# Attention by pairs of key blocks: operations of 1024 columns over two PSUM banks

## The chip, the cores and the metric

The kernel runs on one core of a Trainium2 chip. The metric is the device time of one execution in microseconds (us), as the median of several runs. The core has a matrix engine (PE; its weight loads are shown apart as PEld), a vector engine (DVE), an activation engine (ACT), a general engine (POOL, GpSimd) and a queue for transfers (SP). Each works through its own list of instructions in order; semaphores tie the lists together. On-chip data lie in SBUF; matrix products land in PSUM, which has eight banks of 512 float32 columns on each of 128 partitions.

## The reference

Two layers on 2048 positions of width 1024: a Mamba-2 mixer, then latent attention with 16 heads. The change touches the attention alone:

```python
def causal_block_attention(q_nope, q_rope, k_nope, k_rope, v):
    S = q_nope.shape[1]
    scale = (QK_NOPE + QK_ROPE) ** -0.5        # 64 + 32 columns
    for i in range(S // Q_BLOCK):              # blocks of 128 queries
        ...
        s = einsum(q_nope, k_nope) + einsum(q_rope, k_rope)
        s = s.astype(jnp.float32) * scale
        mask = (q0 + local)[:, None] >= jnp.arange(kv_len)[None, :]
        p = jax.nn.softmax(jnp.where(mask, s, -jnp.inf), axis=-1).astype(v.dtype)
        outs.append(jnp.einsum('bhqk,bkhd->bqhd', p, v[:, :kv_len]))
```

Everything is float32 there. The kernel carries each operand as two float16 values, a high and a low half, and adds the products that matter.

## The kernel before

The stage works on 64 jobs: 16 heads, and in each the four quarters of 512 queries (`qb` = 0 to 3). The quarter `qb` needs 4*qb + 4 blocks of 128 keys. There are two passes over the scores.

*Maxima.* `maxima` (L1226) multiplies 128 queries by up to 512 keys, high halves only, into a PSUM bank (L1235), adds the causal mask on the last piece (L1237), and DVE reduces it to a maximum per query (L1238). After the job's last piece DVE forms the bias: the maximum over the pieces (`m`, L1243), its scaling (`me`, L1247), and its high and low half (`nm`, L1249 and L1250). `row` (L1252) turns these on PE (L1255), DVE copies them out (`rT`, L1257), and two transfers put them as two further rows behind the queries, so that the scores of the second pass come out with the maximum subtracted.

*Scores and values.* A unit is one block of 128 keys against the job's 512 queries. `scores` (L1261) makes three products into one bank (L1269 to L1271, high by high, high by low, low by high) and the mask on the diagonal (L1273). ACT takes the exponential (`x`, L1275) and copies it to float16, the high half (`PTs`, L1277). The low half is the difference (L1279): DVE makes it, or POOL in two of five units off the diagonal. `values` (L1282) multiplies, for each of four tiles of 128 queries, the high half by 130 columns (64 of the values' low half, 64 of their high half, 2 constant for the sum; L1291) and the low half by 66 of them (L1293), into two columns ranges of one tile `tr`. `finish` (L1301) runs twice per job: ACT copies one range (`Ot`, L1306), DVE takes the reciprocal of the sum (L1308) and adds the ranges (L1310), POOL multiplies (L1313). `store` (L1318) transposes a finished pair of heads (L1323), and ACT copies it out (L1325).

*What sets the order.* PE's order is written out by the loop at L1342: in each step i as many pieces of `maxima` as `due[i]` asks, then what waits in `later` (`row` after ROWS steps, `store` after TURN steps), then `scores` of unit i, then `values` of the unit HELD steps before. READY says how many units ahead of a job its maxima must be made. The lists of DVE, ACT and POOL are set by a scheduler that works from the same program. PSUM is shared by two groups of four banks: `mm` for maxima, scores, `row` and `store`, and `tr` for the outputs; buffers of a group are taken in turn.

After the stage, `back` (L1366) does the output product; its weight splits (L1383 on ACT, L1384 on POOL) are partly placed inside the attention stage.

Of the kernel before, what the change touches and what calls it, by code (L numbers as in the profile page):

```python
# [27 lines left out]
NH = 16  # L28
# [39 lines left out]
class Net:  # L68
# [1115 lines left out]
    def attention(self):  # L1184
        with ExitStack() as ctx:
            self.wo = self.tail.enter_context(self.tc.tile_pool(name="wo", bufs=1, side="right", reuse_waits="tile"))
            self.wraw = []
            sp = ctx.enter_context(self.tc.tile_pool(name="asp", bufs=2, reuse_waits="tile"))
            with self.tc.manual_schedule(engines={mybir.EngineType.PE}):
                self.heads(sp)  # L1190

    def heads(self, sp):
# [5 lines left out]

        def cuts(kv):

            out, at = [], 0
            while at < kv:
                w = min(TB, kv - at)
                if kv - at == TB + P:
                    w = 384
                out.append((at, w))
                at += w
            return out

        jobs = [(h, qb) for h in range(NH) for qb in range(NB)]  # L1210
        chunks, ends = [], []
        for n, (h, qb) in enumerate(jobs):
            for j in range(4):
                parts = cuts(qb * TB + (j + 1) * P)
                chunks += [(n, j, i, c0, w, i == len(parts) - 1) for i, (c0, w) in enumerate(parts)]
            ends.append(len(chunks))
        units = [(n, kb) for n, (h, qb) in enumerate(jobs) for kb in range(4 * qb + 4)]

        need = [ends[units[min(i + READY, len(units) - 1)][0]] for i in range(len(units))]
        due = list(need)  # L1220
        for i in range(len(units) - 2, -1, -1):
            due[i] = max(due[i], due[i + 1] - (2 if i < 40 and i % 2 else 1))

        peak, outs, pairs = {}, {}, {}

        def maxima(n, j, i, c0, w, last):  # L1226

            h, qb = jobs[n]
            if (j, i) == (0, 0):
                peak[n] = self.t(sp, "mx", [P, 4, 4], bufs=3)  # L1230
# [3 lines left out]
            s = self.t(self.pp, "mm", [P, TB], bufs=4)  # L1234
            mm(s[:, :w], Q[0:96, 0, qs], K[0:96, 0, c0:c0 + w], start=True, stop=not last)  # L1235
            if last:
                mm(s[:, w - P:w], self.idb, self.mk, start=False, stop=True)  # L1237
            v.tensor_reduce(peak[n][:, j, i:i + 1], s[:, :w], AX.X, ALU.max)  # L1238
            if last and j == 3:
                m = peak.pop(n)  # L1240
                if qb:
# [5 lines left out]
                v.tensor_scalar(e, x, -1.0 / MSCALE, LN16 / MSCALE, ALU.mult, ALU.add)  # L1247
                u = turned[n % 2]
                v.tensor_copy(u[:, 0:4], e)  # L1249
                v.tensor_tensor(u[:, 4:8], e, u[:, 0:4], ALU.subtract)  # L1250

        def row(n):  # L1252

            ps = self.t(self.pp, "mm", [P, TB], bufs=4)
            mm(ps[:, 0:P], turned[n % 2], self.idb, start=True, stop=True)  # L1255
            r = self.t(sp, "rT", [8, P], F16, bufs=2)
            v.tensor_copy(r, ps[0:8, 0:P])  # L1257
# [3 lines left out]
        def scores(i):  # L1261

            n, kb = units[i]
            h, qb = jobs[n]
            jj = max(kb - 4 * qb, 0)
            diag = kb >= 4 * qb
            Q, K, ks, c = quer[h, qb], keys[h % 2], slice(kb * P, (kb + 1) * P), slice(jj * P, TB)
            s = self.t(self.pp, "mm", [P, TB], bufs=4)
            mm(s[:, c], K[0:98, 0, ks], Q[0:98, 0, c], start=True, stop=False)  # L1269
            mm(s[:, c], K[0:96, 0, ks], Q[0:96, 1, c], start=False, stop=False)  # L1270
            mm(s[:, c], K[0:96, 1, ks], Q[0:96, 0, c], start=False, stop=not diag)  # L1271
            if diag:
                mm(s[:, jj * P:(jj + 1) * P], self.mk, self.idb, start=False, stop=True)  # L1273
            x = self.t(sp, "x", [P, TB], bufs=4)
            act(x[:, c], s[:, c], AF.Exp)  # L1275
            u = self.t(sp, "PTs", [P, 2, TB], F16, bufs=HELD + 2)
            act(u[:, 0, c], x[:, c], AF.Copy)  # L1277
            engine = nc.gpsimd if not diag and i % 5 in (1, 3) else v
            engine.tensor_tensor(u[:, 1, c], x[:, c], u[:, 0, c], ALU.subtract)  # L1279
            return u  # L1280

        def values(i, u):  # L1282

            n, kb = units[i]
            h, qb = jobs[n]
            V = vals[h % 2]
            if kb == 0:
                outs[n] = [self.t(self.pp, "tr", [P, 2, 256], bufs=4) for _ in range(2)]
            for j in range(max(kb - 4 * qb, 0), 4):
                o, js = outs[n][j // 2][:, j % 2], slice(j * P, (j + 1) * P)  # L1290
                mm(o[:, 0:130], u[:, 0, js], V[:, kb, :], start=kb == 0 and j % 2 == 0, stop=False,  # L1291
                   skip_group_check=True)
                mm(o[:, 64:130], u[:, 1, js], V[:, kb, 64:130], start=False, stop=kb == 4 * qb + j,  # L1293
                   skip_group_check=True)
            if kb in (4 * qb + 1, 4 * qb + 3):
                finish(n, (kb - 4 * qb) // 2)
            if kb == 4 * NB - 1 and h + 2 < NH:
                self.load_k(h + 2, 0, NB)
                self.load_v(h + 2)

        def finish(n, i):  # L1301

            h, qb = jobs[n]
            O = outs[n][i]
            t = self.t(sp, "Ot", [P, 2, 64], bufs=2)
            act(t, O[:, :, 0:64], AF.Copy)  # L1306
            ri = self.t(sp, "ri", [P, 2], bufs=2)
            v.reciprocal(ri, O[:, :, 128])  # L1308
            o = self.t(sp, "Oa", [P, 2, 64], bufs=2)
            v.tensor_tensor(o, O[:, :, 64:128], t, ALU.add)  # L1310
# [4 lines left out]
            if i and h % 2:  # L1315
                later.append((step[0] + TURN, lambda: store(h, qb)))

        def store(h, qb):  # L1318

            op = pairs.pop((h // 2, qb))  # L1320
            ps = self.t(self.pp, "mm", [P, TB], bufs=4)
            for j in range(4):
                nc.tensor.transpose(ps[:, j * P:(j + 1) * P], op[:, j].rearrange("p h d -> p (h d)"), self.ident)  # L1323
            o = self.t(sp, "Os", [P, TB], bufs=2)
# [14 lines left out]
                    later.remove((at, f))  # L1339
                    f()  # L1340

        for i in range(len(units)):  # L1342
            step[0] = i
            while made < due[i]:
                maxima(*chunks[made])
                made += 1
                n = chunks[made - 1][0]
                if made == ends[n]:
                    if i:
                        later.append((i + ROWS, lambda n=n: row(n)))  # L1350
                    else:
                        row(n)
            waiting()
            held.append((i, scores(i)))
            if len(held) > HELD:
                values(*held.pop(0))
        while held:
# [120 lines left out]
    def run(self):  # L1478
        tc = self.tc
        with ExitStack() as whole:  # L1480
            cp = whole.enter_context(tc.tile_pool(name="const", bufs=1))
            dp = whole.enter_context(tc.tile_pool(name="dram", bufs=1, space=DRAM))
            self.pp = whole.enter_context(tc.tile_pool(name="pp", bufs=4, space=PSUM))
# [18 lines left out]
            self.wo_d = dp.tile([G, 2, 2, P, 2, 2, TB], F16, name="wo_d")  # L1502
            self.xq = whole.enter_context(tc.tile_pool(name="xq", bufs=8, side="right"))
            self.layers()
            self.attention()
            self.back()
            self.tail.close()


# [48 lines left out]
```

## Time and profile before

| | |
|---|---|
| median of 3 runs | 3019.27 us (3012.62 to 3020.14) |
| the profiled run's own time | 3012.66 us |
| its span | 3010.9 us |
| attention stage, about | 2008 to 2824 us of the span |
| busy in the whole span | PE 95%, DVE 76%, ACT 63%, POOL 22% |
| granted clock over the span | 0.987 |

The profile is of one execution; what lies around its span is 1.8 us. Times in rows are microseconds from the span's start. A row of the timeline has start, duration, engine, line, operation, out<-in, the tile's shape, and in brackets the idle time before it with what ended it. Instructions of one engine overlap at their ends, so from start to start is less than the duration. A group of the page or of a window gives busy time and the mean in ns of one, then idle time ahead with its releasers. For PE the row's end is modelled; the starts are what to subtract.

### The profile page before, as it was taken

What the parts mean: (1) busy time and instruction counts of PE and PEld (TensorE: products, weight loads), DVE (VectorE), ACT (ScalarE), POOL (GpSimd) and SP (SyncE); (2) the same over time, 40 slices, a digit from 0 to 9 for tenths busy, and PEclk for the clock granted to TensorE, in tenths of its full rate; (3) what the DMA queues carried; (4) which work ended last, traced back from release to release, by engine and by line L of the source; (5) the groups of instructions that cost most, each with busy time, mean ns of one, the idle gap of its engine ahead of it and who ended that gap; (6) DMA issues with size and microseconds to landing.
All of it is one profiled execution on the core that took longest, in us unless ns stands there. A gap on an engine that the chain in (4) does not pass through costs nothing.

```text
span 3010.9 us, 55172 instructions
## 1 busy us (share of the span) xinstructions
PE 2871.6 (95%) x19726; PEld 1686.8 (56%) x19726; DVE 2281.5 (76%) x5162; ACT 1885.9 (63%) x4360; POOL 665.7 (22%) x798
## 2 busy tenths in 40 slices
PE   7899999999999999999999999989999999998998
PEld 3456656555555554544555454545666656665787
DVE  6789987787877788787855544368988989898554
ACT  8777666665766666565543433338888888887622
POOL 0212122121222112221111212113232323234200
PEclk9999999999999999999999999999999999999999
DMA  8765435544464456455357555631212121222462
GB/s 284 241 227 179 155 116 196 175 154 141 168 212 157 145 175 198 172 165 186 123 162 262 176 167 194 201 96 43 62 43 69 43 62 43 69 64 74 141 210 105
DMA packets 234248, 440.70 MB, mean 146 GB/s; under 512 B 59218, under 2 KB 101010, under 8 KB 232532
## 3 DMA queue, kind: packets, MB, share of 16 engines
q1 hardware_dynamic: 222836, 401.24, 41.9%
q0 software_dynamic: 11136, 35.92, 3.3%
q8 instruction: 155, 2.54, 0.3%
q14 instruction: 121, 0.99, 0.1%
HBM read 332.73 MB, written 104.34 MB: 145 GB/s over the span
## 4 chain that ended last, share of the span: by engine, by line
PE 60%; DVE 19%; ACT 10%; issue 6%; DMA 4%; POOL 1%; SPq 0%; ACTq 0%; DVEq 0%; POOLq 0%
PE mm L84 11%; PE mm L86 11%; PE mm L85 11%; PE tr L85 4%; PE tr L84 4%; PE tr L86 4%; DVE cacc L612 4%; ACT x L1275 3%; DVE PTs L1279 3%; DVE mx L1238 3%; ACT PTs L1277 2%; PE mm L1269 2%; PE mm L1270 2%; PE mm L1271 2%; PE tr L1291 2%
## 5 line engine op out<-in xcount | busy, mean ns | idle before, releaser
L1275 ACT ACTIVATE x<-mm 128x512 f32<-128x512 f32 (+3 forms) x640 | 336.1, 525 | 124.9 <-PE mm L1271 59.2
L1238 DVE TENSOR_REDUCE mx<-mm 128x1 f32<-128x512 f32 (+3 forms) x640 | 378.4, 602 | 39.3 <-PE mm L1237 23.4
L1277 ACT ACTIVATE PTs<-x 128x512 f16<-128x512 f32 (+3 forms) x640 | 361.7, 566 | 16.2
L1279 DVE TENSOR_TENSOR PTs<-x,PTs 128x512 f16<-128x512 f32 (+3 forms) x512 | 306.9, 604 | 45.3 <-ACT PTs L1277 35.2
L84 PE MATMUL mm<-xT,wsp 128*128 128x512 f16 x800 | 306.7, 383 | 6.3 <-ACT wsp L115 4.2
L85 PE MATMUL mm<-xT,wsp 128*128 128x512 f16 x800 | 305.7, 382 | 0.0
L86 PE MATMUL mm<-xT,wsp 128*128 128x512 f16 x800 | 305.3, 382 | 0.0
L1291 PE MATMUL tr<-K,PTs 128*128 128x130 f16 x2176 | 280.0, 222 | 0.0
L1293 PE MATMUL tr<-K,PTs 128*128 128x66 f16 x2176 | 260.5, 194 | 9.0 <-POOL PTs L1279 6.2
L1291 PEld LDWEIGHTS <-PTs 128*128 128x128 f16 x2176 | 203.8, 98 | 61.4 <-issue 4.5
L84 PE MATMUL mm<-wsp,xT 128*128 128x512 f16 (+1 forms) x640 | 230.3, 361 | 4.7 <-ACT craw L606 4.5
L85 PE MATMUL mm<-wsp,xT 128*128 128x512 f16 (+1 forms) x640 | 230.5, 360 | 3.2 <-DVE wsp L116 3.2
L612 DVE SCALAR_TENSOR_TENSOR cacc<-craw,pack,cacc 128x512 f32<-128x512 f32 x288 | 214.1, 771 | 24.2 <-ACT cacc L610 23.2
L1269 PE MATMUL mm<-xT,K 98*128 98x512 f16 (+3 forms) x640 | 227.2, 355 | 4.3 <-DVE mx L1238 3.4
L1293 PEld LDWEIGHTS <-PTs 128*128 128x128 f16 x2176 | 197.7, 98 | 59.7 <-POOL PTs L1279 7.9
L86 PE MATMUL mm<-wsp,xT 128*128 128x512 f16 (+1 forms) x640 | 230.5, 360 | 0.0
L1270 PE MATMUL mm<-xT,K 96*128 96x512 f16 (+3 forms) x640 | 227.1, 355 | 0.0
L1235 PE MATMUL mm<-K,xT 96*128 96x512 f16 (+3 forms) x640 | 225.2, 358 | 1.1 <-DVE Xp L116 1.1
L1271 PE MATMUL mm<-xT,K 96*128 96x512 f16 (+3 forms) x640 | 225.6, 352 | 0.0
L802 POOL TENSOR_TENSOR Xp<-Xw,Xp 128x512 fp32r<-128x512 f32 x64 | 89.6, 1400 | 499.6 <-ACT Xp L801 280.5
L84 PE MATMUL mm<-wsp,yT 128*128 128x512 f16 (+1 forms) x512 | 197.5, 386 | 2.2 <-DVE sz L636 1.6
L86 PE MATMUL mm<-wsp,yT 128*128 128x512 f16 (+1 forms) x512 | 195.8, 382 | 0.0
(461 smaller groups left out, 6946.9 us busy)
## 6 DMA issues: line engine op xcount, KB each, us to landing
wsp<-wi_d SPq DMA_DIRECT2D x96, 512.0 KB
big<-cumT SPq DMA_DIRECT2D x64, 512.0 KB
wraw<-in_ssm_w_out_dram SPq DMA_DIRECT2D x96, 256.0 KB
wi_d<-wsp SPq DMA_DIRECT2D x32, 512.0 KB
wsp<-wo_d SPq DMA_DIRECT2D x32, 512.0 KB
wsp<-wu_d SPq DMA_DIRECT2D x28, 512.0 KB
hx<-in_ssm_w_in_dram SPq DMA_DIRECT2D x48, 256.0 KB
wraw<-in_ssm_w_in_dram SPq DMA_DIRECT2D x48, 256.0 KB
```

The lines of the kernel that those rows point to most:

```text
L84: mm(out, l_hi, r_hi, start=start, stop=False)
L85: mm(out, l_hi, r_lo, start=False, stop=False)
L86: mm(out, l_lo, r_hi, start=False, stop=stop)
L612: nc.vector.scalar_tensor_tensor(acc, raw[:, k:k + TB], wk[k], acc, ALU.mult, ALU.add)
L1238: v.tensor_reduce(peak[n][:, j, i:i + 1], s[:, :w], AX.X, ALU.max)
L1269: mm(s[:, c], K[0:98, 0, ks], Q[0:98, 0, c], start=True, stop=False)
L1270: mm(s[:, c], K[0:96, 0, ks], Q[0:96, 1, c], start=False, stop=False)
L1275: act(x[:, c], s[:, c], AF.Exp)
L1277: act(u[:, 0, c], x[:, c], AF.Copy)
L1279: engine.tensor_tensor(u[:, 1, c], x[:, c], u[:, 0, c], ALU.subtract)
L1291: mm(o[:, 0:130], u[:, 0, js], V[:, kb, :], start=kb == 0 and j % 2 == 0, stop=False, skip_group_check=True)
L1293: mm(o[:, 64:130], u[:, 1, js], V[:, kb, 64:130], start=False, stop=kb == 4 * qb + j, skip_group_check=True)
```

## The change

A unit becomes a pair of key blocks. The two blocks' scores lie in two neighbouring banks, the second block's pushed to the start of its bank so that the columns are contiguous, and Exp and Copy run once over up to 1024 columns. The low half of the first block is made by DVE, that of the second by POOL, in every pair. Maxima are reduced over up to 1024 columns, so a job has one piece or two per 128 queries. The value product of 130 columns becomes one of 64 and one of 65, all three now accumulating into the same 65 columns; `finish` runs once per job, with a reciprocal and one multiplication by DVE out of PSUM. PSUM in this stage is three buffers of two banks (`s`, for maxima, scores, `row`, `store`) and two banks for outputs (`o`). HELD, READY, ROWS and TURN count pairs now. The bank groups before and after the stage are opened apart.

```diff
-HELD = 3
-READY = 7
-ROWS = 2
-TURN = 4
+HELD = 2
+READY = 4
+ROWS = 1
+TURN = 2
...
         def cuts(kv):
-            out, at = [], 0
-            while at < kv:
-                w = min(TB, kv - at)
-                if kv - at == TB + P:
-                    w = 384
...
+            first = kv if kv <= 2 * TB else TB if kv <= 3 * TB else 2 * TB
+            return [(0, first)] + ([(first, kv - first)] if kv > first else [])
...
-            due[i] = max(due[i], due[i + 1] - (2 if i < 40 and i % 2 else 1))
+            due[i] = max(due[i], due[i + 1] - (3 * TB if i < 20 else 2 * TB))
...
+        def bank():
+            return self.t(self.ap, "s", [P, 2, TB], bufs=3)
...
-                    v.tensor_reduce(x, m[:, :, :qb + 1], AX.X, ALU.max)
+                    v.tensor_tensor(x, m[:, :, 0], m[:, :, 1], ALU.max)
...
+            x = self.t(sp, "x", [P, 2 * TB], bufs=3)
+            act(x[:, at:end], s, AF.Exp)
+            u = self.t(sp, "PTs", [P, 2, 2 * TB], F16, bufs=HELD + 2)
+            act(u[:, 0, at:end], x[:, at:end], AF.Copy)
+            v.tensor_tensor(u[:, 1, at:TB], x[:, at:TB], u[:, 0, at:TB], ALU.subtract)
+            nc.gpsimd.tensor_tensor(u[:, 1, TB:end], x[:, TB:end], u[:, 0, TB:end], ALU.subtract)
...
-                mm(o[:, 0:130], u[:, 0, js], V[:, kb, :], start=kb == 0 and j % 2 == 0, stop=False,
-                   skip_group_check=True)
-                mm(o[:, 64:130], u[:, 1, js], V[:, kb, 64:130], start=False, stop=kb == 4 * qb + j,
-                   skip_group_check=True)
+                    hi, lo = u[:, 0, at:at + P], u[:, 1, at:at + P]
+                    mm(o[:, 0:64], hi, V[:, k, 0:64], start=k == 0 and j == 0, stop=False, skip_group_check=True)
+                    mm(o[:, 0:65], hi, V[:, k, 64:129], start=False, stop=False, skip_group_check=True)
+                    mm(o[:, 0:65], lo, V[:, k, 64:129], start=False, stop=k == 4 * qb + j, skip_group_check=True)
...
-            act(t, O[:, :, 0:64], AF.Copy)
...
-            nc.gpsimd.tensor_tensor(pairs[h // 2, qb][:, 2 * i:2 * i + 2, h % 2, :], o,
-                                    ri.unsqueeze(2).to_broadcast([P, 2, 64]), ALU.mult)
+            v.reciprocal(ri, O[:, :, 64])
+            v.tensor_tensor(pairs[h // 2, qb][:, :, h % 2, :], O[:, :, 0:64],
+                            ri.unsqueeze(2).to_broadcast([P, 4, 64]), ALU.mult)
```

What it does to the engines' lists, at three places. First PE, one query tile's value products before:

```order
L1291 LDWEIGHTS PTs_22211
L1291 MATMUL tr_22104<-K_3813_20590,PTs_22211 128x130
L1293 LDWEIGHTS PTs_22211
L1293 MATMUL tr_22104<-K_3813_20590,PTs_22211 128x66
L1291 LDWEIGHTS PTs_22211
L1291 MATMUL tr_22104<-K_3813_20590,PTs_22211 128x130
```

and after the change (line numbers of the changed kernel):

```order
L1299 LDWEIGHTS PTs_22034
L1299 MATMUL o_22075<-K_3813_20590,PTs_22034 128x64
L1300 LDWEIGHTS PTs_22034
L1300 MATMUL o_22075<-K_3813_20590,PTs_22034 128x65
L1301 LDWEIGHTS PTs_22034
L1301 MATMUL o_22075<-K_3813_20590,PTs_22034 128x65
```

Two loads and two products have become three and three, the high half being loaded twice. Second DVE, from the last maximum of a fourth quarter to the copy of its row, before (L1238 maximum, L1243 to L1250 the bias, L1279 a low half, L1257 the copy):

```order
L1238 TENSOR_REDUCE mx_23663<-mm_24007 128x1
L1243 TENSOR_REDUCE m_24011<-mx_23663 128x4
L1247 TENSOR_SCALAR me_24013<-m_24011 128x4
L1238 TENSOR_REDUCE mx_24034<-mm_24039 128x1
L1249 CAST nm_4004_21660<-me_24013 128x4
L1250 TENSOR_TENSOR nm_4004_21660<-me_24013,nm_4004_21660 128x4
L1279 TENSOR_TENSOR PTs_24023<-x_24021,PTs_24023 128x512
L1238 TENSOR_REDUCE mx_24034<-mm_24060 128x1
L1257 CAST rT_24066<-mm_24064 8x128
```

and after, where the maximum is L1240, the bias L1245 to L1252, low halves L1282, the quarter's end L1313 and L1316, the copy L1259:

```order
L1282 TENSOR_TENSOR PTs_23774<-x_23772,PTs_23774 128x512
L1313 RECIPROCAL ri_23825<-o_23692 128x4
L1316 TENSOR_TENSOR Op_23827<-o_23692,ri_23825 128x4x64
L1240 TENSOR_REDUCE mx_23549<-s_23829 128x1
L1282 TENSOR_TENSOR PTs_23812<-x_23810,PTs_23812 128x512
L1245 TENSOR_TENSOR m_23834<-mx_23549 128x4
L1249 TENSOR_SCALAR me_23836<-m_23834 128x4
L1251 CAST nm_4004_21664<-me_23836 128x4
L1252 TENSOR_TENSOR nm_4004_21664<-me_23836,nm_4004_21664 128x4
L1259 CAST rT_23880<-s_23878 8x128
```

A low half stands between the last maximum and the bias now, and no maximum of the next job inside the bias. Third DVE, at a first quarter's four maxima, before:

```order
L1238 TENSOR_REDUCE mx_24034<-mm_24060 128x1
L1257 CAST rT_24066<-mm_24064 8x128
L1238 TENSOR_REDUCE mx_24034<-mm_24087 128x1
L1279 TENSOR_TENSOR PTs_24076<-x_24074,PTs_24076 128x512
L1238 TENSOR_REDUCE mx_24034<-mm_24109 128x1
L1279 TENSOR_TENSOR PTs_24098<-x_24096,PTs_24098 128x512
L1247 TENSOR_SCALAR me_24113<-mx_24034 128x4
```

and after:

```order
L1282 TENSOR_TENSOR PTs_23893<-x_23891,PTs_23893 128x512
L1282 TENSOR_TENSOR PTs_23932<-x_23930,PTs_23932 128x512
L1240 TENSOR_REDUCE mx_23999<-s_24004 128x1
L1282 TENSOR_TENSOR PTs_23971<-x_23969,PTs_23971 128x256
L1240 TENSOR_REDUCE mx_23999<-s_24008 128x1
L1240 TENSOR_REDUCE mx_23999<-s_24012 128x1
L1240 TENSOR_REDUCE mx_23999<-s_24016 128x1
L1249 TENSOR_SCALAR me_24020<-mx_23999 128x4
```

The four maxima, which were spread among the low halves of four units, now come in one step, with the last low half of the job before between the first and the second.

More of the change, by code (lines that the diff above doesn't have):

```diff
@@ L1233, in maxima @@
             Q, K, qs = quer[h, qb], keys[h % 2], slice(j * P, (j + 1) * P)
[L1234 to L1237, printed above, removed]
+            s = bank().rearrange("p a b -> p (a b)")
+            for at in range(0, w, TB):
+                c = min(TB, w - at)
+                diag = last and at + c == w
+                mm(s[:, at:at + c], Q[0:96, 0, qs], K[0:96, 0, c0 + at:c0 + at + c], start=True, stop=not diag)
+                if diag:
+                    mm(s[:, w - P:w], self.idb, self.mk, start=False, stop=True)
             v.tensor_reduce(peak[n][:, j, i:i + 1], s[:, :w], AX.X, ALU.max)
@@ L1264, in scores @@
             h, qb = jobs[n]
[L1265 to L1279, printed above, removed]
-            return u
-        def values(i, u):
-            n, kb = units[i]
+            Q, K, s = quer[h, qb], keys[h % 2], bank()
@@ L1504, in run @@
             self.layers()
+            banks.close()
             self.attention()
+            self.pp = banks.enter_context(tc.tile_pool(name="pe", bufs=4, space=PSUM, reuse_waits="tile"))
             self.back()
+            banks.close()
             self.tail.close()
```

89 lines of the change are left out of this document (50 added, 39 removed).

## The prediction

> **What bounds the kernel now.** I read the busy times of the attention stage first, then the waits, then single rows. The change touches only this stage, so its stretch is what counts (columns: stretch, length, busy time and instructions of PE, PEld, DVE, ACT, POOL, granted clock, DMA share, GB/s).
>
> ```profile
> 2010.00:2824.00 814.00, 743.74 (x7581) 484.74 (x7579) 724.31 (x1689) 683.69 (x1447) 250.05 (x262) 0.97 0.22 54
> ```
>
> PE 91%, DVE 89%, ACT 84%: no engine is clear of the next. The table of waits (engine, line, releaser: us, times, longest) says which wait ends last:
>
> ```profile
> PEld L1255 <- DVE nm L1250: 68.4, 62, 2.5
> PE mm L1255 <- DVE nm L1250: 52.7, 47, 2.2
> PE tr L1293 <- POOL PTs L1279: 6.2, 4, 2.1
> PE mm L1269 <- DVE mx L1238: 3.4, 10, 0.6
> ```
>
> PE stops almost only at `row`, L1255, for the DVE chain that turns the row maxima into biases: 68.4 us from the weights' side, 4.3 us per head. Nothing else stops it for long. The clock of 0.97 costs about 3% of 814, 24 us. The rest is PE's own work, so time comes from shorter PE work, shorter stops, or a steadier clock. These PE rows give its prices and the worst stop:
>
> ```profile
> 2330.52 0.38 PE L1269 MATMUL mm<-xT,K 98*128 98x512 f16 x1
> 2330.74 0.38 PE L1270 MATMUL mm<-xT,K 96*128 96x512 f16 x1
> ...
> 2338.69 0.22 PE L1291 MATMUL tr<-K,PTs 128*128 128x130 f16 x1
> 2338.75 0.19 PE L1293 MATMUL tr<-K,PTs 128*128 128x66 f16 x1
> 2338.78 0.22 PE L1291 MATMUL tr<-K,PTs 128*128 128x130 f16 x1
> ...
> 2339.04 0.33 PE L1235 MATMUL mm<-K,xT 96*128 96x384 f16 x1
> ...
> 2315.61 0.38 PE L1235 MATMUL mm<-K,xT 96*128 96x512 f16 x1
> 2318.08 0.23 PE L1255 MATMUL mm<-idb,nm 128*128 128x128 bf16 x1 [2.08 <-DVE nm L1250]
> ```
>
> 512 columns take 0.22 from start to start. Four value pairs of 130 and 66 columns take 2339.04 - 2338.69 = 0.35, 87 ns each, of which the short product is 0.03. Before 2318.08 PE stood 2.25 us beyond its last product's 0.22: DVE has other work between the links of the bias chain there.
>
> **The change, part by part.**
>
> *Short products.* Per block and query tile 130 + 66 columns become 64 + 65 + 65, each with its own weight load (2176 more pairs of load and product). At 29 ns each three are 87 ns: no change; by rounding +1 ns, +2 us. Ends: 57 ns each, the gap of the 130-column product, would add 2176 x (171 - 87) = +183 us; nothing makes them cheaper than 194/196 of now (-2 us). I take +2, since 66 columns with a load before them are measured and 64 or 65 are the nearest thing to them. The Trainium skill, "TensorE: Matmul & The Clock Gate", Back-to-back issue gap, gives about 81 ns for each load-and-product pair of 128 columns in a stream; by it 6528 pairs would be bound by loads and the sum some 2176 x 81 = 176 us higher. The trace has 57 ns at 130 columns, so the trace does not agree, and it stands only in the third rival.
>
> *ACT.* Two Exp and two Copy of 512 become one each of 1024.
>
> ```profile
> L1277 ACT ACTIVATE PTs<-x 128x512 f16<-128x512 f32 x448 | 282.1, 630 | 10.7
> L1275 ACT ACTIVATE x<-mm 128x512 f32<-128x512 f32 x447 | 263.9, 591 | 72.3 <-PE mm L1271 59.2 <-DVE PTs L1279 7.2 <-PE mm L1273 3.3
> L1277 ACT ACTIVATE PTs<-x 128x128 f16<-128x128 f32 x64 | 19.8, 309 | 2.0
> L1383 ACT ACTIVATE W<-wr 128x1024 fp32r<-128x1024 f32 x4 | 4.2, 1052 | 0.0
> L1306 ACT ACTIVATE Ot<-tr 128x128 f32<-128x128 f32 x128 | 34.6, 271 | 0.3 <-PE tr L1293 0.3
> ```
>
> From 128 to 512 columns a Copy grows by 321 ns, so 512 more columns cost 0.43 and 1024 take 1.06 (the 1024-wide row says 1.05); an Exp likewise about 1.02. One pair of blocks then holds ACT for 2.0 instead of 2.3 us: 320 x 0.3 = 96 us, and Ot's 35 go too. But of PE's waits for ACT the view shows less than 1 us, so this is worth nothing by itself. What it does is lengthen each link: from scores to low halves an Exp and a Copy now last 2.1 us instead of 1.2.
>
> *DVE.* 640 maxima become 384.
>
> ```profile
> L1238 DVE TENSOR_REDUCE mx<-mm 128x1 f32<-128x512 f32 x392 | 264.2, 682 | 15.4 <-PE mm L1235 14.6 <-PE mm L1237 0.3
> L1279 DVE TENSOR_TENSOR PTs<-x,PTs 128x512 f16<-128x512 f32 x320 | 226.6, 708 | 34.4 <-ACT PTs L1277 26.8 <-ACT x L1275 0.3
> L1279 POOL TENSOR_TENSOR PTs<-x,PTs 128x512 f16<-128x512 f32 x128 | 149.5, 1168 | 192.2 <-issue 110.3 <-ACT PTs L1277 74.1 <-PE tr L1293 4.1
> 2334.48 0.68 DVE L1238 TENSOR_REDUCE mx<-mm 128x1 f32<-128x512 f32 x1
> 2335.08 0.68 DVE L1279 TENSOR_TENSOR PTs<-x,PTs 128x512 f16<-128x512 f32 x1
> ```
>
> A 512-wide maximum is 0.68, and the next operation starts 0.60 after it did. One of 128 columns lasts 0.28 (further below), so a column costs 1.05 ns and one of 1024 columns holds DVE 1.14. Fewer starts save 256 x 0.07 = 18 us. The low halves lose what POOL takes over, and the outputs are finished in one piece. In sum about 4 us per head leave DVE: again only worth what it does to the stop.
>
> *POOL and the SBUF port.* Now POOL takes the second block's low half of every pair (320 instead of 128 operations), and DVE the first block's, both released by the same Copy. Before, unmasked blocks were divided between them in turn. Here are rows where the two met late in the stage:
>
> ```profile
> 2709.70 1.28 DVE L1279 TENSOR_TENSOR PTs<-x,PTs 128x512 f16<-128x512 f32 x1 [1.08 <-ACT PTs L1277]
> 2711.51 1.03 DVE L1279 TENSOR_TENSOR PTs<-x,PTs 128x512 f16<-128x512 f32 x1
> ...
> 2708.08 2.35 POOL L1384 TENSOR_TENSOR W<-wr,W 128x1024 fp32r<-128x1024 f32 x1 [1.46 <-ACT W L1383]
> 2710.40 1.60 POOL L1279 TENSOR_TENSOR PTs<-x,PTs 128x512 f16<-128x512 f32 x1
> ```
>
> DVE's low half begins at 2709.70 under POOL's operation and ends at 2710.98, 0.55 after that one does; POOL's next takes 1.60 while DVE finishes, and DVE's next at 2711.51 ends 0.54 after POOL's. They exclude each other: a pair costs POOL's 1.17 plus 0.54 in a row, not side by side. The bias chain is caught the same way:
>
> ```profile
> 2335.50 0.63 ACT L1277 ACTIVATE PTs<-x 128x512 f16<-128x512 f32 x1
> 2336.26 1.16 POOL L1279 TENSOR_TENSOR PTs<-x,PTs 128x512 f16<-128x512 f32 x1 [1.44 <-ACT PTs L1277]
> 2336.60 0.85 DVE L1247 TENSOR_SCALAR me<-m 128x4 f32<-128x4 f32 x1
> 2337.36 0.28 DVE L1238 TENSOR_REDUCE mx<-mm 128x1 f32<-128x128 f32 x1
> 2337.56 0.15 DVE L1249 CAST nm<-me 128x4 f16<-128x4 f32 x1
> 2337.75 0.16 DVE L1250 TENSOR_TENSOR nm<-me,nm 128x4 f16<-128x4 f32 x1
> ```
>
> A four-column operation lasts 0.85, to POOL's end at 2337.42; reductions out of PSUM pass freely. The Trainium skill's "GPSIMD Engine Reference", Specifications, says that GpSimd shares its SBUF interfaces with VectorE and contends with instructions that have two SBUF inputs; the rows agree, 1.60 beside 1.16. That rule speaks against this change.
>
> In the steady middle of a quarter this fits: PE needs 0.44 + 1.31 + 0.70 = 2.45 us per pair, the port 1.7, and the maximum runs under POOL. At the ends of jobs it does not. I laid the new orders out by hand over one head, starting each instruction at its releaser's end plus the gaps above (Copy's end at 2336.13 to POOL's start 0.13, a dependent DVE step 0.2, and by estimate 0.2 from the last score product's turn to Exp). Two places:
>
> Row of the fourth quarter: time 0 is the last maxima product. PE reaches `row` after 0.49 + 1.30 (scores) + 0.70 (values) = 2.5. On DVE, between the last maximum and the bias stands a low half. Its scores ended at -0.26 (nine short products before time 0), so Exp runs from -0.06 and Copy ends at 2.05; POOL takes its half from 2.18 to 3.34. DVE had to wait for POOL in the previous pair until 0.89, then needs 0.53 for that half, 0.53 for finishing the quarter before and 1.14 for the maximum: free at 3.09, it waits for POOL and ends at 3.87; four dependent steps of 0.2 give 4.7. PE waits 2.2, or 1.7 where the low half goes first by 0.1 us. By the same count: first quarter 0, second and third 1.3 each. Rows thus cost 4.3 to 4.8 per head, about as before: the shorter DVE work is eaten by the port.
>
> Score buffers: four single-bank buffers become three of two banks, and `row` and `store` take whole ones. At the first quarter's four maxima, which come together, the fourth product needs the first's buffer and the scores the second's; in DVE's order the second maximum stands behind a low half that waits for its Copy and POOL: 1.0 us. Then two pairs that wait for maxima (0.6 and 0.3), two that wait until DVE has copied `row`'s buffer, behind another low half (0.45 and 0.47), and two smaller ones of 0.3: together 3.4 per head. Before, the waits show 3.4 us for such buffers in the whole stage; that is the lower end, the upper is 3.4 more per head if all ties go wrong.
>
> *The rest.* The end of the stage gains 3 us: no product on POOL before the last transposes, and fewer starts on ACT. POOL's weight splits (L1384, above) now always stand before a low half; before, values waited 6.2 us for POOL, and I keep that. DMAs are the same in number; `row` to first scores keeps 6 us of PE work (5.4 before, where nothing waited; both counted in the order at the prices above), so this stays hidden; if it did not, each late job would cost the remainder. The clock I leave at 0.97: stops of about 2 us remain one per head.
>
> Sum: +2 (products) + 16 x (3.4 + 0 to 0.5 - 0.3 for small waits now gone) = +50 to +58, - 3 (end): +49 with ties in its favour. The profiled run took 3012.66, so 3062. That run stands 6.6 below the median of 3019.27, at the lowest of the three; I add 2 for that: **3064**.
>
> **Rivals.** *The port is dodged* (faster). DVE is lighter, so if it idles when a Copy ends, its half goes first by 0.09 us; POOL's late end then hides behind the two pairs held back, and bias and buffers come early. For it: DVE has 4 us less per head. Against: a 1.14 us maximum is in its way in most pairs. The same layout without the port gives rows of 0, 0.5, 0.7 and 1.1 us, 2.3 per head, and buffer waits of 2; with no stop near 2 us the clock would recover some 20: 16 x (4.3 - 4.3 - 0.3) - 20 + 2 - 3 = -26, about 2989 with the same 2 for the runs, and less where buffers come early too. It decides when POOL goes first in fewer than about a third of the pairs.
>
> *Nothing on the path moves* (same). ACT and DVE save beside PE, and new buffer waits equal what rows lose: 3012 to 3019. For it: the ends of jobs are few; against: waits of 3.4 per head would have to vanish exactly into 3.4 saved.
>
> *Short products do not stream* (slower still). Eight triples in a row, with a load each, are not in the trace. Each ns over 29 costs 6.5 us; at 35 ns it is +39, near 3100; at 57 each it is +183, near 3250. Against: the 0.03 rows above. The 81 ns that the Trainium skill gives for a stream of loads and products lies at that end; I leave 0.01 of this case's chance for it.
>
> **How the numbers follow.** First case 0.63 (own range 3030 to 3105), dodged port 0.22 (2955 to 3005), nothing moves 0.10, slow products 0.05. A change under 0.3%, 9 us, cannot be told from none. The same case gives 0.08 of same and 0.01 to each side. Faster 0.23, same 0.08, slower 0.69. For 8 in 10 the range reaches into the second case, to 2970, and up to 3115 (all ties wrong: 16 x 3.4, +54).
>
> **What would show it.** Right: DVE low halves of 512 columns far above 0.71 on average, or POOL's above 1.17; PE idle before `row` of at least 60 us; PE idle before scores and maxima released by DVE of some 50; ACT near 70% busy. Short products right: 0.03 apart. Wrong: low halves at 0.69 and 1.16, `row` waits under 40 us, clock 1.0. What would undo the forecast is above all the order in which DVE and POOL reach the port.

## The result and the profile after

The changed kernel takes 3086.66 us (median of 4 runs, 3084.15 to 3087.62) against 3018.21 for the kernel before (median of 4 as well, a fourth run of 3017.15 being added to the three above): ratio 1.0229, interval 1.0211 to 1.0246, 68 us slower. The forecast was 3064, the range 2970 to 3115. The profiled run took 3085.92, its span is 3084.0; the span grew by 73.1 us, 71 of them in the attention stage. Its stretch, in the columns of the prediction's first fence:

```profile
2010.00:2896.00 886.00, 774.11 (x9771) 501.52 (x9770) 691.95 (x1108) 598.06 (x681) 415.92 (x327) 0.97 0.19 50
```

PE is at 87% instead of 91, DVE at 78 instead of 89, ACT at 67.5 instead of 84; only POOL has more (250 to 416 us). PE, DVE and ACT each stand idle for longer, and POOL is busy for less than half of the stage (47%), so the stage waits for chains and not for a full engine. The waits in that stretch:

```profile
PEld L1257 <- DVE nm L1252: 89.4, 47, 7.9
PE s L1257 <- DVE nm L1252: 73.9, 46, 7.8
...
PE s L1272 <- DVE mx L1240: 18.7, 33, 0.8
...
PE s L1237 <- ACT x L1279: 5.3, 15, 0.4
...
PE s L1237 <- DVE mx L1240: 3.7, 16, 0.2
...
PE s L1272 <- DVE rT L1259: 3.0, 14, 0.2
```

`row` (L1257 now) is still the worst, 89.4 instead of 68.4 us from the weights' side, and scores and maxima (L1272, L1237) now wait for buffers. These idle times count from a product's modelled end; from start to start the same stops are longer. So I worked the stage out from the starts, from about 2009 us to its last product (2824 and 2896): each gap less the undisturbed spacing of the same product (0.216 us at 512 columns, 0.056 at 128, 0.029 at 64). Half speed means stretches in which products come at twice that spacing; the granted clock is 0.5 there. Where the stage is cut, and where a stop ends and half speed begins, moves a row by up to 4 us.

| us in the stage | before | after | difference | forecast |
|---|---|---|---|---|
| products at their spacing, with gaps under 0.07 | 710.8 | 720.0 | +9.2 | +2 |
| stops before `row` | 67.2 | 82.6 | +15.4 | 0 to +8 |
| other stops | 19.9 | 58.1 | +38.2 | +50 |
| excess where products run at half speed | 17.9 | 26.0 | +8.1 | 0 |
| stage | 815.7 | 886.8 | +71.1 | +49 |

The end's forecast of -3 is in no row of its own. "Other stops" forecast: 16 x (3.4 - 0.3). The low halves by shape, L1283 POOL's and L1282 DVE's, and the wide ACT and DVE operations:

```profile
L1283 POOL TENSOR_TENSOR PTs<-x,PTs 128x512 f16<-128x512 f32 x192 | 291.0, 1516 | 358.4 <-ACT PTs L1281 180.0 <-DVE mx L1240 93.7 <-PE s L1257 64.2
L1282 DVE TENSOR_TENSOR PTs<-x,PTs 128x512 f16<-128x512 f32 x256 | 231.0, 902 | 107.7 <-ACT PTs L1281 99.0 <-PE o L1301 4.6 <-POOL PTs L1283 3.3
L1281 ACT ACTIVATE PTs<-x 128x1024 f16<-128x1024 f32 x192 | 202.8, 1056 | 6.0
L1279 ACT ACTIVATE x<-s 128x1024 f32<-128x1024 f32 x192 | 196.5, 1023 | 201.0 <-PE s L1274 149.0 <-issue 28.7 <-DVE mx L1240 20.4
L1240 DVE TENSOR_REDUCE mx<-s 128x1 f32<-128x1024 f32 x112 | 136.4, 1218 | 29.3 <-PE s L1237 17.8 <-PE s L1239 9.7
```

At 512 columns DVE's low half takes 902 ns on average instead of 708, POOL's 1516 instead of 1168: they hold each other up. How that reaches PE is seen at a fourth quarter's `row`:

```profile
2251.68 0.38 PE L1274 MATMUL s<-xT,K 96*128 96x512 f16 x1
...
2252.60 0.19 PE L1301 MATMUL o<-K,PTs 128*128 128x65 f16 x1
2255.62 0.29 PE L1257 MATMUL s<-idb,nm 128*128 128x128 bf16 x1 [2.83 <-DVE nm L1252]
2255.70 0.63 PE L1272 MATMUL s<-xT,K 98*128 98x512 f16 x1
2256.13 0.63 PE L1273 MATMUL s<-xT,K 96*128 96x512 f16 x1
...
2251.07 1.21 DVE L1240 TENSOR_REDUCE mx<-s 128x1 f32<-128x1024 f32 x1
2252.29 0.69 DVE L1282 TENSOR_TENSOR PTs<-x,PTs 128x512 f16<-128x512 f32 x1
2252.90 1.11 DVE L1245 TENSOR_TENSOR m<-mx 128x4 f32<-128x4 f32 x1
2254.05 0.17 DVE L1249 TENSOR_SCALAR me<-m 128x4 f32<-128x4 f32 x1
2254.25 0.17 DVE L1251 CAST nm<-me 128x4 f16<-128x4 f32 x1
2254.45 1.11 DVE L1252 TENSOR_TENSOR nm<-me,nm 128x4 f16<-128x4 f32 x1
...
2252.32 1.67 POOL L1283 TENSOR_TENSOR PTs<-x,PTs 128x512 f16<-128x512 f32 x1 [0.70 <-DVE mx L1240]
2254.39 1.15 POOL L1283 TENSOR_TENSOR PTs<-x,PTs 128x512 f16<-128x512 f32 x1 [0.40 <-ACT PTs L1281]
```

DVE's low half starts 0.03 ahead of POOL's and goes first (0.69), POOL's takes 1.67. Then `m`, four columns, lasts until POOL's end at 2253.99; the next two links take 0.17 each because POOL is free; the last link starts 0.06 behind POOL's next operation and lasts again 1.11, to that one's end. PE stands 2.99 us beyond the last product's spacing, of which the two held links are about 1.9. After it the products come every 0.43 us, at half speed. This is no single case: `m` is held in all 16 fourth quarters (1.09 us on average) and the last link in 14 of them (1.11), each to within 0.03 us of the end of POOL's operation, and neither is held in any other quarter, where they take 0.16.

### The profile page after: what moved, and what is told of

Read it like the earlier page. It is cut to its first block, busy times and chain, and to the rows that moved or that the text cites. A ratio compares the mean times of both kernels' runs of the same rounds, so it can differ in the third digit from the quotient of the medians.

```text
span 3084.0 us, 58360 instructions
## 1 busy us (share of the span) xinstructions
PE 2902.4 (94%) x21902; PEld 1705.3 (55%) x21902; DVE 2244.6 (73%) x4570; ACT 1801.0 (58%) x3592; POOL 828.1 (27%) x862
## 4 chain that ended last, share of the span: by engine, by line
PE 57%; DVE 19%; ACT 6%; issue 4%; DMA 3%; POOL 1%; SPq 0%; ACTq 0%; DVEq 0%; POOLq 0%
PE mm L84 10%; PE mm L86 9%; PE mm L85 9%; DVE mx L1240 4%; DVE PTs L1282 4%; PE tr L85 3%; PE tr L84 3%; PE tr L86 3%; DVE cacc L612 3%; PE s L1272 3%; PE s L1273 3%; PE s L1274 3%; PE s L1237 2%; ACT x L1279 2%; PE tr L879 1%
## 5 line engine op out<-in xcount | busy, mean ns | idle before, releaser
L1283 POOL TENSOR_TENSOR PTs<-x,PTs 128x512 f16<-128x512 f32 (+1 forms) x320 | 401.5, 1257 | 472.2 <-ACT PTs L1281 234.9
L1279 ACT ACTIVATE x<-s 128x1024 f32<-128x1024 f32 (+1 forms) x320 | 285.6, 892 | 283.7 <-PE s L1274 149.0
L1240 DVE TENSOR_REDUCE mx<-s 128x1 f32<-128x1024 f32 (+7 forms) x384 | 341.5, 904 | 63.0 <-PE s L1239 41.7
L1282 DVE TENSOR_TENSOR PTs<-x,PTs 128x512 f16<-128x512 f32 x320 | 269.3, 848 | 112.8 <-ACT PTs L1281 103.2
L1281 ACT ACTIVATE PTs<-x 128x1024 f16<-128x1024 f32 (+1 forms) x320 | 297.0, 928 | 10.0
L1272 PE MATMUL s<-xT,K 98*128 98x512 f16 (+3 forms) x640 | 229.3, 358 | 22.4 <-DVE mx L1240 18.7
L1301 PE MATMUL o<-K,PTs 128*128 128x65 f16 x2176 | 240.4, 195 | 4.0 <-POOL PTs L1283 2.0
L1300 PE MATMUL o<-K,PTs 128*128 128x65 f16 x2176 | 240.6, 196 | 0.0
L1299 PE MATMUL o<-K,PTs 128*128 128x64 f16 x2176 | 240.6, 194 | 0.0
L1273 PE MATMUL s<-xT,K 96*128 96x512 f16 (+3 forms) x640 | 229.5, 359 | 0.0
L1274 PE MATMUL s<-xT,K 96*128 96x512 f16 (+3 forms) x640 | 228.3, 357 | 0.0
L1299 PEld LDWEIGHTS <-PTs 128*128 128x128 f16 x2176 | 206.8, 99 | 29.2 <-issue 3.4
L1300 PEld LDWEIGHTS <-PTs 128*128 128x128 f16 x2176 | 205.4, 99 | 24.8 <-issue 3.2
L1301 PEld LDWEIGHTS <-PTs 128*128 128x128 f16 x2176 | 204.6, 100 | 6.1 <-POOL PTs L1283 3.2
```

Of the source, the lines that this page charges most:

```text
L1272: mm(o, K[0:98, 0, ks], Q[0:98, 0, c], start=True, stop=False)
L1273: mm(o, K[0:96, 0, ks], Q[0:96, 1, c], start=False, stop=False)
L1279: act(x[:, at:end], s, AF.Exp)
L1282: v.tensor_tensor(u[:, 1, at:TB], x[:, at:TB], u[:, 0, at:TB], ALU.subtract)
L1283: nc.gpsimd.tensor_tensor(u[:, 1, TB:end], x[:, TB:end], u[:, 0, TB:end], ALU.subtract)
L1299: mm(o[:, 0:64], hi, V[:, k, 0:64], start=k == 0 and j == 0, stop=False, skip_group_check=True)
```

## The experiments

Ratios are to the kernel before on the same chip. The theory throughout: POOL's operation in every pair excludes DVE's from what the prediction calls the port (its rows show that the two exclude each other), and through the bias chain and the buffers this stops PE. Its rivals: the buffers and links of the new form are to blame, DVE's load is, or the short products.

**1. The short products alone**, in the kernel before:

```diff
-                mm(o[:, 0:130], u[:, 0, js], V[:, kb, :], ...)
+                mm(o[:, 0:64], u[:, 0, js], V[:, kb, 0:64], ...)
+                mm(o[:, 64:130], u[:, 0, js], V[:, kb, 64:130], ...)
                 mm(o[:, 64:130], u[:, 1, js], V[:, kb, 64:130], ...)
```

> The kernel before with one part of the change alone: the value product of 130 columns split into 64 and 66 columns, each with its own weight load, so 2176 more loads and products. In the trace after the change three short products take 91 ns from start to start of the next three, before a pair takes 86.6: if these 4.5 ns are the price, +10 us (3028, 1.003); by the forecast's term, +2 us (3020); if loads bound a stream of short products, +150 us or more.

3027.32, ratio 1.0025 (1.0015 to 1.0036): 4.5 to 11 us. The price of about 4.5 ns per triple (9.8 us) lies inside the interval, the forecast's +2 is too small, and a bound by loads is out.

**2. POOL's low half left out.**

```diff
-            nc.gpsimd.tensor_tensor(u[:, 1, TB:end], x[:, TB:end], u[:, 0, TB:end], ALU.subtract)
-                    hi, lo = u[:, 0, at:at + P], u[:, 1, at:at + P]
+                    hi, lo = u[:, 0, at:at + P], u[:, 0 if b else 1, at:at + P]
```

> The changed kernel without POOL's low half of the second block: that block's low product takes the high half instead, so PE, ACT and DVE have the same instructions, POOL has none in a pair, and the output lacks those low halves. Theory (the port): DVE's low halves fall from 0.90 to about 0.71 us at 512 columns, the bias chain is never held by POOL, PE's stops fall from about 8.4 us per head (5.1 before `row`, 3.3 for score buffers) to about 4.3, as the layout without the port gave: 3087 - 16 x 4.1 = 3021, between 3010 and 3040. Rival (three buffers of two banks, longer links from scores to low halves, and the order of DVE set the stops; the port adds little): stops fall by less than 1 us per head, 3070 to 3087.

2992.31, ratio 0.9908 (0.9894 to 0.9921): 94 us less than after the change, more than the theory's 66 and below its range. Its waits in the stage, with PE idle before `row` down from 73.9 to 20.5:

```profile
PEld L1257 <- DVE nm L1252: 34.0, 39, 6.7
...
PE s L1257 <- DVE nm L1252: 20.5, 32, 6.6
PE s L1272 <- DVE mx L1240: 14.0, 33, 0.6
```

And DVE's low halves in its groups by shape:

```profile
L1282 DVE TENSOR_TENSOR PTs<-x,PTs 128x512 f16<-128x512 f32 x256 | 177.9, 695 | 88.2 <-ACT PTs L1281 85.8
```

At 695 ns they take less than before the change. Worked out from the starts, stops before `row` fall from 82.6 to 28.3, other stops from 58.1 to 41.9, half speed from 26.0 to 5.1. The two kinds of stops fell by 70 in sum, a little more than expected; half speed was not in the sum at all. Other stops stay 22 us above the kernel before: that part is there without POOL's operation, and the runs do not divide it between buffers, links and order.

**3. The same operation on POOL, set aside.** The run before takes from POOL both the port and the values' wait for its result. This one gives the port back alone:

```diff
+            idle = self.t(sp, "idle", [P, TB], F16, bufs=2)
+            nc.gpsimd.tensor_tensor(idle[:, 0:end - TB], x[:, TB:end], u[:, 0, TB:end], ALU.subtract)
```

> As the run without POOL's low half (second blocks' low product takes the high half, so the output lacks those low halves; 2992), but POOL makes the same subtraction from the same inputs at the same place and writes it into a tile that nothing reads. PE no longer depends on POOL; POOL and DVE still meet. Theory (the port): DVE's low halves are back at about 0.90 us at 512 columns, POOL's at 1.5, the bias chain is held again, and the time is near that of the change, 3065 to 3090. Rival (the run without POOL gained because the values' low halves came without POOL's 1.2 us): 2990 to 3010.

3085.83, ratio 1.0226 (1.0201 to 1.0251), the time of the change. In its groups by shape (L1284 is the operation set aside):

```profile
L1284 POOL TENSOR_TENSOR idle<-x,PTs 128x512 f16<-128x512 f32 x192 | 288.5, 1503 | 362.5 <-ACT PTs L1281 362.4
L1282 DVE TENSOR_TENSOR PTs<-x,PTs 128x512 f16<-128x512 f32 x256 | 234.4, 916 | 111.7 <-ACT PTs L1281 104.2 <-PE o L1302 3.7 <-POOL idle L1284 2.2
```

An operation whose result nobody reads costs the whole 94 us, and stops PE as the change does (before `row` 82.9, others 56.7, half speed 31.1). That is the port, since PE has nothing to wait for from POOL here; ACT and DVE wait for buffers that POOL still reads for 4.9 us in all.

**4. POOL copies instead of subtracting** (the low halves of second blocks are then left out):

```diff
-            nc.gpsimd.tensor_tensor(u[:, 1, TB:end], x[:, TB:end], u[:, 0, TB:end], ALU.subtract)
+            nc.gpsimd.tensor_copy(u[:, 1, TB:end], x[:, TB:end])
```

> The changed kernel with POOL's subtraction replaced by a copy of the same columns (one input from SBUF instead of two; the low halves of second blocks are then wrong values). Theory: what counts is DVE's two inputs, POOL holds the port with any operation; if the copy lasts about as long as the subtraction, DVE's low halves stay at 0.85 to 0.95 us and the time between 3060 and 3090. Rival: only two operations with two inputs each exclude each other; DVE's low halves fall to about 0.70 and the time to 2990 to 3005, as without POOL.

3008.14, ratio 0.9972 (0.9963 to 0.9981). Neither time was met, since the copy is not like the subtraction, as its group by shape shows:

```profile
L1283 POOL CAST PTs<-x 128x512 f16<-128x512 f32 x192 | 119.0, 620 | 417.5 <-ACT x L1279 417.5
```

And rows of its timeline where a copy meets the bias chain:

```profile
2317.38 0.51 POOL L1283 CAST PTs<-x 128x384 f16<-128x384 f32 x1 [2.50 <-ACT x L1279]
...
2317.23 0.17 DVE L1249 TENSOR_SCALAR me<-m 128x4 f32<-128x4 f32 x1
2317.43 0.48 DVE L1251 CAST nm<-me 128x4 f16<-128x4 f32 x1
```

It takes 620 ns, and starts after Exp, while ACT still makes the high half, so it rarely meets DVE's low half. Where it meets a link of the bias chain it holds it, 0.48 instead of 0.17, to the copy's end at 2317.89. So a copy with one input excludes a cast with one input just so: 29 of the stage's 62 casts begin under a copy and last 0.53 us on average, the others 0.17. Stops before `row` are about 43 us, 14 more than without POOL's operation, nearly the whole difference of 16 between the two runs. The time itself tells only that a short operation at another moment costs less.

**5. Both low halves on DVE**, one operation of up to 1024 columns:

```diff
-            v.tensor_tensor(u[:, 1, at:TB], x[:, at:TB], u[:, 0, at:TB], ALU.subtract)
-            nc.gpsimd.tensor_tensor(u[:, 1, TB:end], x[:, TB:end], u[:, 0, TB:end], ALU.subtract)
+            v.tensor_tensor(u[:, 1, at:end], x[:, at:end], u[:, 0, at:end], ALU.subtract)
```

> The changed kernel with both low halves as one DVE operation of up to 1024 columns and none on POOL; the computation is complete. Theory (the port): the operation takes about 1.2 us, less than POOL's 1.17 and DVE's 0.53 in a row, so stops shrink although DVE gets more work (692 us of busy time in the stage less 49 of waiting plus 160: about 800 of 860): about 2.4 us less stop per head, 3048, between 3030 and 3070. Rival (DVE's load is what counts and POOL relieves it): DVE is full at about 2.3 us per pair against PE's 2.45, each stop grows by the 0.5 us that each low half gains, 3095 or more.

3104.11, ratio 1.0279 (1.0259 to 1.0299): the rival's side. Its waits in the stage:

```profile
PEld L1257 <- DVE nm L1252: 87.3, 48, 5.1
...
PE s L1257 <- DVE nm L1252: 72.1, 48, 5.0
```

And the joint operation in its groups by shape:

```profile
L1282 DVE TENSOR_TENSOR PTs<-x,PTs 128x1024 f16<-128x1024 f32 x192 | 236.5, 1232 | 79.9 <-ACT PTs L1281 77.6
```

Without the port, 1.23 us in front of the bias costs as much: stops before `row` 79.9 (82.6), other stops 63.6 (58.1), half speed 47.9 (26.0). So POOL is no mistake as such: what stands between the last maximum and the bias costs PE, be it work or a held port. DVE is busy for 80% of the stage here, so it is not full as the rival had it; whether a later `row` would free this form too, no run shows.

**6. `row` one pair later**, in the changed kernel:

```diff
-READY = 4
-ROWS = 1
+READY = 5
+ROWS = 2
```

> The changed kernel with ROWS 2 and READY 5: maxima are made one pair earlier and `row` stands two steps behind them, so that as much PE work as now lies between `row` and its scores. If the stops before `row` are the delay of one chain (DVE and POOL keep up on average), the 5.1 us per head nearly vanish: 3087 - 16 x 4.5 = 3015, between 3000 and 3035. If DVE and POOL together cannot keep pace, the stops only move, to scores and maxima that wait for buffers: 3070 or more.

2987.87, ratio 0.9893 (0.9880 to 0.9907): 99 us less, and better than the kernel before. Its waits, then POOL's group by shape, then the stage's stretch:

```profile
PE s L1272 <- DVE mx L1240: 18.6, 23, 1.2
PEld L1257 <- DVE nm L1252: 18.0, 43, 3.8
...
PE s L1257 <- DVE nm L1252: 12.5, 25, 3.6
```

```profile
L1283 POOL TENSOR_TENSOR PTs<-x,PTs 128x512 f16<-128x512 f32 x192 | 305.9, 1594 | 271.2 <-ACT PTs L1281 143.1 <-DVE mx L1240 66.4 <-PE s L1326 17.0
```

```profile
2010.00:2800.00 790.00, 750.33 (x9773) 491.39 (x9774) 659.36 (x1109) 598.09 (x682) 436.63 (x327) 0.99 0.22 56
```

POOL's 1594 ns show that the port is as contested as ever, but PE seldom waits for it: stops before `row` are 18.0, other stops 46.4, half speed 6.6. The engines keep up on average, and the stops were the delay of a chain.

**7. `row` two units later**, in the kernel before:

```diff
-READY = 7
-ROWS = 2
+READY = 9
+ROWS = 4
```

> The kernel before with ROWS 4 and READY 9: `row` two units (2.4 us of PE work) later behind its maxima, maxima two units earlier. Its stops before `row` are 67 us in the stage, the longest 2.25, and 10 stretches of 3.3 us at half the clock cost some 16. If those stops are the delay of one chain, nine tenths of them and the half-clock stretches go: 3019 - 60 - 16 = 2943, between 2930 and 2965, and the pairs then cost about 45 us even with `row` late (2988). Rival: DVE at 89% cannot keep up, the stops move to maxima and scores: 2995 or more, and the pairs with `row` late are at least as good.

2974.38, ratio 0.9862 (0.9845 to 0.9878), 44 us less than the kernel before. The stops before `row` go (67.2 to 5.1), half speed falls from 17.9 to 5.9, but other stops rise from 19.9 to 54.6. Its waits show 1.4 us for the bias, and scores (L1269) that wait for their buffer instead:

```profile
PE mm L1269 <- ACT x L1275: 10.9, 27, 0.6
PE mm L1269 <- DVE mx L1238: 7.1, 15, 0.7
...
PE mm L1255 <- DVE nm L1250: 1.4, 8, 0.2
```

2943 was expected; I had counted nothing for the buffers. Compared with the pairs at the same place of `row`, its stage is 778.0 instead of 791.2: the pairs cost 13 us there, 7.9 of it products and small gaps, as in the first experiment.

**8. One unit later:**

```diff
-READY = 7
-ROWS = 2
+READY = 8
+ROWS = 3
```

> The kernel before with ROWS 3 and READY 8: `row` one unit (1.2 us of PE work) later instead of two. With two (2974) the stops before `row` fell from 67 to 5 us, but other stops, for buffers, rose from 20 to 55. If the earlier maxima cause that, one unit keeps about 16 us of row stops (the third quarter's 2.25 less 1.2), no half-clock stretches, and buffer stops near 30: 2962, between 2955 and 2970. If not, 2975 to 2990.

2976.59, ratio 0.9864 (0.9838 to 0.9890), no better than two, and not the 2962 that was expected. Stops before `row` are 26.6, other stops 37.7, in sum 64 against 60: the two trade against each other nearly one for one.

**9. The first quarter's maxima spread.** The first attempt left all four in one step, in both kernels (one early head of the changed kernel apart), since the bound already lay past the third:

```diff
+        for n, (h, qb) in enumerate(jobs):
+            i = next(i for i, d in enumerate(due) if d >= cols[ends[n]])
+            if qb == 0 and i:
+                due[i - 1] = max(due[i - 1], cols[ends[n] - 2])
```

> The changed kernel with the first quarter's four maxima in two steps, two and two, the first two one pair earlier. After the change PE stops there for 0.22, 0.40 and 0.91 us per head for buffers that DVE has not read yet. If the coming together is the cause, 1.0 to 1.5 us per head go: 3087 - 20 = 3067, between 3060 and 3073. Rival: three buffers are too few wherever the maxima stand, the stop moves to the next pair: 3080 or more.

> Both: ROWS 2 and READY 5, and the first quarter's maxima in two steps. With `row` late alone (2988) the stops at these maxima are down to 0.3 us per head, but scores wait 0.9 to 1.4 us per head behind a `row`, in the steps of the first quarters. If these come from the same crowding, 0.5 to 1.0 us per head go: 2976, between 2970 and 2982; else no change, 2983 to 2992.

3088.65 (ratio 1.0244) and 2985.66 (0.9900): repeats of the change and of experiment 6, which tell nothing of the maxima. With the bound at the third's end the first two do move:

```diff
-            i = next(i for i, d in enumerate(due) if d >= cols[ends[n]])
+            i = next(i for i, d in enumerate(due) if d > cols[ends[n] - 1])
```

> The changed kernel with the first quarter's four maxima in two steps; now the bound is set so that the first two do stand one pair earlier (in the earlier attempt all four had stayed in one step, and its time of 3089 is that of the change). 1.0 to 1.5 us per head of buffer stops go: 3067, between 3060 and 3073. Rival: three buffers are too few wherever these maxima stand: 3080 or more.

> ROWS 2 and READY 5 with the first quarter's maxima in two steps, now with effect. Stops at these maxima and at the scores behind that `row` are 1.2 to 1.7 us per head with `row` late alone (2988): 0.5 to 1.0 of them go, 2976, between 2970 and 2982. Else no change, 2983 to 2992.

3077.98, ratio 1.0201 (1.0172 to 1.0229), and 2994.51, ratio 0.9922 (0.9899 to 0.9946). The first lies between what was expected and what the rival gave, and its interval still overlaps that of the change. In it other stops fell from 58.1 to 43.1, 0.9 us per head, nearly as expected, and the stops at these maxima fell from 1.5 to about 0.2 us per head, so the crowding is their cause; but half speed rose from 26.0 to 35.7 and took most of it back. In the second nothing was gained: other stops 49.2, before `row` 22.6.

## Why the prediction was right, and where it was off

**The mechanism** (the port, through the bias chain and in part through buffers) is shown by experiments 2 and 3. The range reached from faster to slower, so the time alone would have told little. The dodged port was priced at 2989; without POOL's operation the kernel takes 2992, and its parts agree as well: against the kernel before, stops before `row` change by -39 us (-32 counted), other stops by +22 (+27), half speed by -13 (-20). That rival lost because POOL went first in 143 of 320 pairs (45%), more than the third that the forecast named.

**Short products**: mis-sized. The rows at 0.03 were right (29 to 30 ns at the median), but a triple takes 91 ns, not 87, at the median (a pair 86 to 87): about 10 us over 2176, where +2 was taken. The rounding of a two-decimal view hid it.

**Score buffers**: right in sum, by luck in the parts. At the first quarter's maxima 0.22, 0.40 and 0.91 us stand where 1.0 was counted; then 0.63 at scores that wait for a maximum (0.9 counted in two places), 0.38 at scores that wait for `row`'s buffer (0.92 counted in two places), and 0.51 at maxima that wait for an Exp, which the forecast does not name: 3.05 per head against 3.4. The rest of the 58 us stands at the stage's two ends. The rise in the table is 12 us below the forecast because the kernel before already had 19.9 us of such stops from start to start, where 0.3 per head, about 5, was subtracted. The view of waits shows only some 25 of the 50 us that were named as its sign, since the modelled ends cover about 0.16 of each stop.

**Rows**: forecast 0, 1.3, 1.3 and 1.7 to 2.2 for the four quarters; in the steady heads 0, 1.04, 1.34 and 2.78 (the second has 0.82 and 1.26 in alternate heads, the fourth 2.57 and 2.99). The step that failed is the fourth quarter's: the layout let the low half wait for POOL and gave the links 0.2 each. In the trace the low half went first, for which the forecast had its lower value, 1.7; but the links themselves were held, two of them by 0.95 each. The forecast had shown such a link at 0.85 and then gave it no price. Nor did `m` get a price for becoming an operation with two inputs (L1245). Before, it was a reduction of one: of 47, 28 began under a POOL operation and lasted 0.17 us on average, the others 0.15, at most 0.17, so it was never held. No run puts the reduction back. The port had its share before as well: there `me` began under a POOL operation in 43 of 62 jobs and lasted 0.70 us on average instead of 0.16. How much of the 67 us of stops that cost, no run shows.

**The end**: no gain. The values' 6.2 us for POOL are down to 2.0, but a `row` at 2814 stops PE for 7.9 us: DVE's chain stands behind a DVE operation of 2.75 us of the next stage (L1402), then meets one of POOL's weight splits of over 2 us. POOL's low halves are not its main cause: without them a `row` still waits 6.6.

```profile
2811.31 2.27 DVE L1249 TENSOR_SCALAR me<-m 128x4 f32<-128x4 f32 x1
...
2811.22 2.33 POOL L1387 TENSOR_TENSOR W<-wr,W 128x1024 fp32r<-128x1024 f32 x1
```

**Clock**: left at 0.97, which is what the stretch shows to two digits; but the half-speed excess rose by 8 us, which a longer stage hides in a mean. **ACT and DVE**: both fell, off the path, as said; Exp and Copy from 697.8 to 582.6 us, 115 where 96 was counted.

So for the stage +49 was too low by 22: 7 on products, 8 on the clock, 18 on rows and the end, less 12 on buffers. (The prediction's "+50 to +58" leaves out the 2 of the products; its +49 has them.)

## What to carry to other kernels

Count what stands in the chain that PE waits for, link by link, and for each link ask which engine's long operation can hold it; a four-column operation costs what it waits for (0.16 us free, 1.1 held). If engines keep up on average, try moving the waiter before making the work cheaper: two numbers in the schedule were worth 99 us after the change and 44 before it. Judge an edit with the waiter moved as well: the 68 us of the pairs shrink to about 13 there (2987.87 against 2974.38).

## What was not expected of the hardware

Half speed follows long stops, so that a stop is paid for twice. From 2050 us to the end of the stage, 14 of the 15 stops of 2.5 us or more in the changed kernel were followed by products at doubled spacing, most often for 3.4 us and three times for twice as long, and none of 21 stops of 1.2 to 1.35 was; before, 12 of 17 stops of 2.1 to 2.4. A stretch of 3.4 us loses 1.7. Around the `row` shown above, in the columns of the prediction's first fence:

```profile
2251.90:2255.30 3.40, 0.89 (x25) 0.77 (x23) 3.29 (x6) 2.33 (x3) 2.58 (x2) 1.00 0.00 0
2255.30:2258.70 3.40, 3.08 (x15) 1.44 (x16) 1.14 (x3) 0.15 (x1) 0.24 (x1) 0.51 0.01 1
...
2262.10:2265.50 3.40, 3.14 (x66) 2.66 (x64) 1.14 (x3) 2.77 (x4) 1.53 (x2) 0.99 0.11 31
```

The length of a stop alone does not decide. With both low halves on DVE, stops of 1.24 to 1.3 came in twos, 1.7 us apart, eight times, and seven of these were followed by half speed, but none of 19 single stops of 1.2 to 1.3. The kept traces narrow it down: in each of the 14 runs the granted clock changes on a grid of 3.413 us. Of 3201 full-speed windows of these grids in the stage, 3059 were idle for less than half (with products counted at their spacing), and none of them was followed by a window at half speed; of 58 that were idle for 0.50 to 0.65 of their length, 43 were followed by one; of 84 that were idle for more, all were. So what counts is the idle time inside one window, and a stop that an edge of the grid divides may go free: the one of 2.57 us at 2870 did.

The Trainium skill, "TensorE: Matmul & The Clock Gate", Part 1, has the clock go to half after an idle window of about 3.4 us, in free-running windows; the grid and the length of the stretches agree, and if the window is read as idle throughout, the condition does not, since stops of 2.6 us amid running products sufficed.
